# Placing matmul operands on a 256-byte grid, with the block products' stationary weights 64 bytes further

## Chip, core and metric

The kernel runs on one core of a Trainium2 chip. The metric is the device time of one execution in microseconds; the time given for the kernel before is the median of three runs.

## What is computed

One decoder layer in float32 on 512 tokens of width 1024: a half-step SwiGLU FFN (hidden width 2816), a token mixer (sparse attention beside dilated sliding-window attention, gated), and a second half-step FFN, each between RMS norms:

```python
def swiglu(x, w_gate, w_up, w_down):
    return (jax.nn.silu(x @ w_gate) * (x @ w_up)) @ w_down
...
        h = rms_norm(x, ffn1_pre[l])
        x = x + 0.5 * rms_norm(swiglu(h, ffn1_w_gate[l], ffn1_w_up[l], ffn1_w_down[l]), ffn1_post[l])
        h = rms_norm(x, mix_pre[l])
        y = token_mixer(h, w_in[l], nsa_pe_k[l], nsa_w_ck1[l], nsa_w_ck2[l], nsa_pe_v[l],
                        nsa_w_cv1[l], nsa_w_cv2[l], w_nsa_o[l], w_dil_o[l], w_mix_out[l])
        x = x + rms_norm(y, mix_post[l])
        h = rms_norm(x, ffn2_pre[l])
        x = x + 0.5 * rms_norm(swiglu(h, ffn2_w_gate[l], ffn2_w_up[l], ffn2_w_down[l]), ffn2_post[l])
```

## The kernel before

Every float32 product is made of three faster ones. A matrix is split into a rounded part (hi, of type float32r) and a rest (lo); `mm3` then adds hi x hi, hi x lo and lo x hi into one PSUM bank. These are the three lines L409, L410 and L411 of the profile, one matmul each with a weight load (LDWEIGHTS, the row PEld) of its own. The split of weights costs a cast on ScalarE (L380, whi <- raw) and a subtraction on VectorE (L387, wlo <- raw,whi), both 128 x 1024.

`wpair` hands out the split weights' places: three buffers each of tags whi and wlo, used in turn, 4096 bytes a partition. `wsplit` takes a pair and issues the split. Activations and some weights live in slots (x, ring, W, PT, NN, Q, KA and so on) of 2048 or 4096 bytes, and in xh and xl.

The FFN's two first products are computed two blocks of 128 hidden columns at a time (`strassen`, 9 times in the first FFN and 10 times in the second): VectorE forms sums of weight blocks (L645 to L656, into tmp or raw), and seven block products follow, each on weights from `block` and each of 2 x 4 `mm3` with 256 moving columns (`product`), that is 24 matmuls. In them the weights (whi, wlo) are stationary and the tokens (xh, xl, or sums of them in NN, N, PT, CB) move. In the down projections and in the mixer's projection of its output (`ffn_down`, `down`) the activations are stationary and whi and wlo move, 512 columns at a time or, in some products of the mixer, 256. In the remaining projections the weights are stationary and 256 or 512 token columns move.

VectorE also forms sums of the down projection's weights between the block products (L758). The order of all instructions on each engine is written out by hand in a table (`ORDER`), and the tables `HOMES` say which buffer of a tag each use takes. Weights come in by DMAs on SP's queue into three raw buffers.

The pool places each tile at its first use, one after another in steps of 32 bytes in a partition. The small tiles ss, rs and rs2 (4 bytes a partition, for the norms; eight, four and four buffers) were first used between larger ones, and so moved the larger ones off a common place. In the built program the start addresses modulo 256 bytes are:

| tile | before | after |
|---|---|---|
| x, raw, xh, xl, SP, ring, W, NN, N, PT, CB, V, KB, Q, KA, of | 160 | 160 |
| whi, wlo buffer 0 | 96 | 160 |
| whi, wlo buffer 1 | 160 | 160 |
| whi, wlo buffer 2 | 32 | 160 |
| whi, wlo as `block` uses them | 96, 160, 32 | 224 |
| tmp | 96 | 160 |

Column blocks of 128 elements are 512 bytes, so a place modulo 256 holds for all k and j of a tile.

Of the kernel before, what the change touches and what calls it, by code (L numbers as in the profile page):

```python
# [13 lines left out]
F32 = mybir.dt.float32  # L14
F32R = mybir.dt.float32r
# [7 lines left out]
P = 128  # L23
# [164 lines left out]
HOMES = dict(  # L188
    x=(
        "0765432107654321076543120756431207564312075643120756431207563421706534217065342170653421"  # L190
    ),
    raw=(
        "021021021021021021021021021021021021021021021201201210212101201201201202102102102102102102102102"
        "10210210210210210210210210210"
    ),
    SP=(
# [6 lines left out]
    ss=(  # L203
        "076512347056124371023417052643714073150427136540"
    ),
    rs=(
        "031203120312031203120312"
    ),
    rs2=(
        "031203120312031203120312"  # L210
    ),
# [83 lines left out]
            8: ["of"] * 2 + ["V"] * 2, 9: ["KB"] * 4}  # L295
STEPS = (2, 2, 2), (4, 2)
EARLY = 5
HOLD_TAGS = ["W"] * 2 + ["Q"] * 4 + ["KA"] * 2 + ["V"] * 2 + ["CB", "ring"]
PS_BUFS = dict(S=3, T=2, V=1, F=2)
PS_TAGS = [t for t in PS_BUFS for _ in range(PS_BUFS[t])]  # L300
# [7 lines left out]
class Layer:  # L308
    def __init__(self, ctx, tc, a):
        self.tc, self.nc, self.a = tc, tc.nc, a  # L310
        self.pool = ctx.enter_context(tc.tile_pool(name="sb", bufs=1))
        self.psum = ctx.enter_context(tc.tile_pool(name="ps", bufs=1, space=PSUM))
        self.nps = 0
        self.whole = {}
        self.made = {}
        self.consts()

    def behind(self, ins):
        return nullcontext() if ORDER else self.tc.issue_after(ins)
# [43 lines left out]
        self.nc.sync.dma_start(r, src)  # L363
        return r

    def wpair(self, shape):
        n = 1
        for s in shape:
            n *= s
        out = []  # L370
        for tag in ("whi", "wlo"):
            w = self.tile(self.pool, [P, 1024], F32R, tag, tag, 3)[:, :n]
            if len(shape) == 2:
                w = w.rearrange("p (a b) -> p a b", b=shape[1])
            out.append(w)
        return out
# [22 lines left out]
    def ktiles(self, w):  # L399
        return [[v[:, k] for k in range(KT)] for v in w]  # L400

    def wsplit(self, src, shape, behind=None):
        hi, lo = self.wpair(shape)
        self.split(hi, lo, src, behind)
        return hi, lo

# [163 lines left out]
    def ffn(self, n, wg, wu, wd, post, finish, xsrc, tags, nps, aside=None):  # L570
# [10 lines left out]
        def unit(m, f, slots=False):  # L581
            w = {"g": wg, "u": wu}[m]
            if self.pre_split:
                return self.pre_split.pop(0)
            if f % 2 == 0:
                raws[m] = self.raw(w[:, f * P:(f + 2) * P].rearrange("(k p) f -> p k f", p=P), [KT, 2 * P])
            src = raws[m][:, :, (f % 2) * P:(f % 2 + 1) * P]
            if slots:
                return self.wslots(src, "SP", (self.last_cast, self.last_update) if n else None)
            return self.ktiles(self.wsplit(src, [KT, P]))  # L590
# [16 lines left out]

        def block(src):

            return self.wsplit(src, [4, 2 * P])  # L610

        def product(b, w, rhs, start, stop):
            for j in range(2):
# [5 lines left out]
        def strassen(p):  # L619
# [24 lines left out]

            nc.vector.tensor_add(s1, a21, a22)  # L645
            w = block(a11)
            nc.vector.tensor_sub(a21, a11, a21)
            product(r11, w, b11, True, False)
            w = block(a21)
            product(r7, w, t3, True, True)  # L650
            nc.vector.tensor_sub(s2, s1, a11)
            w = block(s2)
            nc.scalar.copy(r12, r11)
            product(r12, w, t2, False, False)
# [27 lines left out]
        for tag, (m, f) in zip(tags, todo):  # L682
            w = unit(m, f, len(first) == 3)
# [32 lines left out]
        for p in range(NF // 2):  # L716
# [26 lines left out]
            hi, lo = [self.slot(tags["E"].pop(0), F32R) for _ in range(2)]  # L743
# [92 lines left out]
    def ffn_down(self, E, X, Y, wd, post, finish, xsrc, defer):  # L836
# [27 lines left out]
        def product(a, wname, banks, start, stop, side=None, tail=0, keep=None, between=None, pre=(), begin=0, end=NP):  # L864


            held = []

            def mm(t, k, w):
                hi, lo = a(k, t)  # L870
                self.mm3(banks[t], hi, lo, w[0], w[1], start and k == 0, stop and k == end - 1, True)

            for k, w in pre:
                for t in range(2):
                    mm(t, k, w)
            for k0 in range(begin, end, 4):
                n = min(4, end - k0)
                r = self.raw(weights[wname](k0, n), [n, S])
                for k1 in range(0, n, 2):
                    m = min(2, n - k1)  # L880
                    if keep and k0 + k1 + m > end - tail:
                        for j in range(m):
                            w = [self.slot(keep.pop(0), F32R) for _ in range(2)]
                            self.split(w[0], w[1], r[:, k1 + j])
                            held.append((k0 + k1 + j, w))
                        continue
                    hi, lo = self.wsplit(r[:, k1:k1 + m], [m, S])
                    for j in range(m):
                        k = k0 + k1 + j
                        if k >= end - tail:  # L890
                            held.append((k, (hi[:, j], lo[:, j])))
                        else:
                            for t in range(2):
                                mm(t, k, (hi[:, j], lo[:, j]))
                        if side:
                            side(k)
            for t in range(2):
                for k, w in held:
                    mm(t, k, w)
                if t == 0 and between:  # L900
                    between()

        def half(lst, off):
            return lambda k, t: [v[:, off + t * P:off + (t + 1) * P] for v in lst[k]]
# [39 lines left out]
        else:  # L944
            nc.sync.dma_start(xl[:, 0:EARLY].bitcast(F32), weights["T4"](0, EARLY))

        def held_sums(k):
            ks = slice(k, min(k + 2, EARLY))
            src = xl[:, ks].bitcast(F32)
            if defer:  # L950
                d4 = self.sbt("tmp", [P, 2, S], bufs=2)[:, 0:ks.stop - k]
                with self.behind(self.last_rest):
                    nc.vector.tensor_sub(d4, xh[:, ks].bitcast(F32), src)
                src = d4
            self.split(xh[:, ks], xl[:, ks], src)

        todo = list(range(0, EARLY, 2))

# [33 lines left out]
        def between():  # L992
            scaled(2, 0, c[0])
            r = self.rstd([ms[2, 0], ms[2, 1]], 2.0)
            while self.pending:
                self.pending.pop(0)()
            update(2, (c[0], c22[0]), r)

        product(half(parts["O"], 256), "T4", c, False, True, None, NP - EARLY, list(HOLD_TAGS), between,
                [(k, (xh[:, i], xl[:, i])) for i, k in enumerate(defer or range(EARLY))],  # L1000
                *((3, NP - 2) if defer else (EARLY, NP)))
        r = self.rstd([self.meansq(c[1], S, 2.0), ms[3, 1]], 2.0)
# [903 lines left out]
```

## Time and profile before

| | |
|---|---|
| median of three runs | 1118.34 us (1118.12 to 1118.46) |
| the profiled execution | 1118.38 us |
| its span, first to last instruction | 1116.3 us |
| TensorE busy | 1107.4 us, 99%, 7070 matmuls |
| VectorE busy | 916.6 us, 82% |
| ScalarE busy | 654.0 us, 59% |
| granted TensorE clock, mean | 0.999 |

Matmuls are pipelined: the duration of one in the profile overlaps the next one's. How fast TensorE gets through a stretch is read from the starts of its matmuls, first to last, divided by their number. A row of the timeline gives start in us, duration in us, engine, line, operation, tiles (out <- operands: the moving one first, the stationary one second), shape and count.

### The profile page before, as it was taken

What the parts mean: (1) busy time and instruction counts of PE and PEld (TensorE: products, weight loads), DVE (VectorE), ACT (ScalarE), POOL (GpSimd) and SP (SyncE); (2) the same over time, 40 slices, a digit from 0 to 9 for tenths busy, and PEclk for the clock granted to TensorE, in tenths of its full rate; (3) what the DMA queues carried; (4) which work ended last, traced back from release to release, by engine and by line L of the source; (5) the groups of instructions that cost most, each with busy time, mean ns of one, the idle gap of its engine ahead of it and who ended that gap; (6) DMA issues with size and microseconds to landing.
All of it is one profiled execution on the core that took longest, in us unless ns stands there. A gap on an engine that the chain in (4) does not pass through costs nothing.

```text
span 1116.3 us, 18832 instructions
## 1 busy us (share of the span) xinstructions
PE 1107.4 (99%) x7070; PEld 1000.2 (90%) x7070; DVE 916.6 (82%) x1569; ACT 654.0 (59%) x1185; POOL 78.8 (7%) x112
## 2 busy tenths in 40 slices
PE   9999999999999999999999999999999999999997
PEld 8899999998889988888888998888999999998886
DVE  7799999988787878987666688976898988879674
ACT  6355555566564777887564725645655555558462
POOL 1000000000002022443000000001000000000001
PEclk9999999999999999999999999999999999999999
DMA  9967676788864562202467768782324334257862
GB/s 294 305 200 243 217 227 191 220 279 284 309 197 119 167 164 85 92 14 71 167 206 263 222 179 289 238 283 95 105 86 130 127 123 133 88 198 239 281 219 81
DMA packets 153952, 207.36 MB, mean 186 GB/s; under 512 B 19939, under 2 KB 98563, under 8 KB 153605
## 3 DMA queue, kind: packets, MB, share of 16 engines
q1 hardware_dynamic: 153856, 206.16, 57.0%
q8 instruction: 55, 0.90, 0.3%
q14 instruction: 37, 0.30, 0.1%
q10 hardware_dynamic: 4, 0.00, 0.0%
HBM read 166.76 MB, written 39.37 MB: 185 GB/s over the span
## 4 chain that ended last, share of the span: by engine, by line
PE 92%; DVE 3%; DMA 2%; ACT 1%; issue 1%; POOL 1%; SPq 0%; DVEq 0%; POOLq 0%; ACTq 0%
PE pb_F L409 12%; PE pb_F L411 12%; PE pb_F L410 11%; PE pb_S L409 8%; PE pb_S L411 8%; PE pb_S L410 8%; PE pb_T L409 6%; PE pb_T L411 6%; PE pb_T L410 6%; PE pb_V L409 3%; PE pb_V L410 3%; PE pb_V L411 3%; PE pb_V L1340 2%; PE pb_T L1325 2%; PE pb_S L1059 1%; DMA raw<-in_w_in_dram 1%
## 5 line engine op out<-in xcount | busy, mean ns | idle before, releaser
L380 ACT CAST whi<-raw 128x1024 fp32r<-128x1024 f32 (+1 forms) x213 | 217.2, 1022 | 246.2 <-issue 75.7
L387 DVE TENSOR_TENSOR wlo<-raw,whi 128x1024 fp32r<-128x1024 f32 (+1 forms) x213 | 252.6, 1188 | 95.0 <-ACT whi L380 86.6
L409 PE MATMUL pb_F<-xh_t,whi 128*128 128x512 f32 (+1 forms) x392 | 142.1, 364 | 0.1
L411 PE MATMUL pb_F<-xh_t,wlo 128*128 128x512 f32 (+1 forms) x392 | 141.2, 362 | 0.2 <-DVE wlo L387 0.2
L410 PE MATMUL pb_F<-xl_t,whi 128*128 128x512 f32 (+1 forms) x392 | 141.1, 362 | 0.0
L380 ACT CAST whi<-tmp_t 128x1024 fp32r<-128x1024 f32 x58 | 60.8, 1049 | 58.2 <-PE pb_S L410 23.0
L387 DVE TENSOR_TENSOR wlo<-tmp_t,whi 128x1024 fp32r<-128x1024 f32 x58 | 70.9, 1222 | 19.5 <-ACT whi L380 18.8
L409 PEld LDWEIGHTS pb_F<-xh_t,whi 128*128 128x128 f32 x392 | 73.9, 189 | 10.0 <-issue 0.3
L411 PEld LDWEIGHTS pb_F<-xh_t,wlo 128*128 128x128 f32 x392 | 73.9, 189 | 9.9 <-DVE wlo L387 0.6
L410 PEld LDWEIGHTS pb_F<-xl_t,whi 128*128 128x128 f32 x392 | 73.9, 189 | 9.0
L409 PE MATMUL pb_S<-xh_t,whi 128*128 128x256 f32 (+1 forms) x232 | 67.3, 290 | 0.0
L411 PE MATMUL pb_S<-xh_t,wlo 128*128 128x256 f32 (+1 forms) x232 | 67.0, 289 | 0.0
L410 PE MATMUL pb_S<-xl_t,whi 128*128 128x256 f32 (+1 forms) x232 | 66.8, 288 | 0.0
L1316 POOL TENSOR_SCALAR SP_s<-SP_s,st_t 128x384 f32<-128x384 f32 (+2 forms) x48 | 49.4, 1043 | 100.6 <-DVE wlo L387 50.8
L431 POOL TENSOR_TENSOR rs_t<-rs_t,mhalf_t 128x1 f32<-128x1 f32 x24 | 15.5, 647 | 536.5 <-DVE rs_t L427 536.0
L411 PE MATMUL pb_T<-xh_t,wlo 128*128 128x256 f32 x184 | 51.7, 283 | 0.0
L410 PE MATMUL pb_T<-xl_t,whi 128*128 128x256 f32 x184 | 51.1, 281 | 0.0
L409 PE MATMUL pb_T<-xh_t,whi 128*128 128x256 f32 x184 | 51.1, 283 | 0.0
L387 DVE TENSOR_TENSOR PT_s<-pb_T,PT_s 128x512 fp32r<-128x512 f32 (+1 forms) x72 | 39.7, 560 | 6.1 <-ACT PT_s L380 5.4
L1065 DVE CUSTOM_DVE_ANT_0 SP_s<-pb_S,W_s 128x128 f32<-128x128 f32 (+2 forms) x92 | 38.7, 444 | 7.3 <-PE pb_S L1060 5.0
L411 PEld LDWEIGHTS pb_S<-xh_t,wlo 128*128 128x128 f32 x232 | 43.8, 189 | 0.7
L409 PEld LDWEIGHTS pb_S<-xh_t,whi 128*128 128x128 f32 x232 | 43.8, 189 | 0.7
(858 smaller groups left out, 3472.0 us busy)
## 6 DMA issues: line engine op xcount, KB each, us to landing
raw<-in_ffn_w_up_dram SPq DMA_DIRECT2D x40, 512.0 KB, 4.4
raw<-in_ffn_w_gate_dram SPq DMA_DIRECT2D x39, 512.0 KB, 4.9
raw<-in_w_in_dram SPq DMA_DIRECT2D x18, 1024.0 KB, 5.5
raw<-in_ffn_w_down_dram SPq DMA_DIRECT2D x14, 1024.0 KB, 5.8
raw<-tdram SPq DMA_DIRECT2D x14, 1024.0 KB, 5.1
NN_s<-in_ffn_w_down_dram SPq DMA_DIRECT2D x22, 512.0 KB, 4.4
tdram<-NN_s SPq DMA_DIRECT2D x22, 512.0 KB, 4.1
odram<-ring_s SPq DMA_DIRECT2D x38, 128.0 KB, 3.3
```

Of the source, the lines that this page charges most:

```text
L380: self.last_cast = self.nc.scalar.copy(dsthi, src).ins
L387: self.last_rest = self.nc.vector.tensor_sub(dstlo, src, dsthi.bitcast(F32)).ins
L409: mm(out, lhi, rhi, start=start, stop=False, skip_group_check=skip)
L410: mm(out, lhi, rlo, start=False, stop=False, skip_group_check=skip)
L411: mm(out, llo, rhi, start=False, stop=stop, skip_group_check=skip)
L431: nc.gpsimd.tensor_tensor(out=r, in0=v, in1=self.mhalf, op=OP.pow)
L1059: mm(out, q[:, qc], ka[:, kc], start=True, stop=False)
L1065: nc.vector.tensor_tensor_reduce(p, s, w, -1.0, FLOOR, OP.add, OP.min, st_m)
L1316: nc.gpsimd.tensor_scalar(pp, pp, st[:, 1, t:t + 1], None, op0=OP.mult)
L1325: nc.tensor.transpose(b[:, o + (t - kk) * P:o + (t - kk + 1) * P], pt[pn][:, po + kk * P:po + (kk + 1) * P], self.ident)
L1340: self.nc.tensor.matmul(out[:, kk * P:S], v, pp, start=first and kk == 0 and pi == 0, stop=False, skip_group_check=True)
```

## The change

The tiles of ss, rs and rs2 are placed first of all. The buffers of whi and wlo are 1088 elements wide in place of 1024 (4352 bytes, 17 times 256), and `block` takes its pair 16 elements (64 bytes) into the buffer. The order of instructions on each engine, their operations and shapes, and their waits are the same as before.

```diff
+SHIFT = 16
...
         self.consts()
+        for tag in ("ss", "rs", "rs2"):
+            for place in sorted(set(HOMES.get(tag, ""))):
+                self.pool.tile([P, 1], F32, name=tag + "_t", tag=tag + place, bufs=1)
...
-    def wpair(self, shape):
+    def wpair(self, shape, shift=0):
...
-            w = self.tile(self.pool, [P, 1024], F32R, tag, tag, 3)[:, :n]
+            w = self.tile(self.pool, [P, 1088], F32R, tag, tag, 3)[:, shift:shift + n]
...
-    def wsplit(self, src, shape, behind=None):
-        hi, lo = self.wpair(shape)
+    def wsplit(self, src, shape, behind=None, shift=0):
+        hi, lo = self.wpair(shape, shift)
...
         def block(src):
-            return self.wsplit(src, [4, 2 * P])
+            return self.wsplit(src, [4, 2 * P], None, SHIFT)
```

## The prediction

> **What bounds the kernel now.** I read the page first (busy shares, granted clock, the chain that ended last), then the table by stretches of 50 us, then the order in time of TensorE alone, to see how far apart its matmuls start.
>
> ```profile
> span 1116.3 us, 18832 instructions
> PE 1107.4 (99%) x7070; PEld 1000.2 (90%) x7070; DVE 916.6 (82%) x1569; ACT 654.0 (59%) x1185; POOL 78.8 (7%) x112
> PEclk9999999999999999999999999999999999999999
> PE 92%; DVE 3%; DMA 2%; ACT 1%; issue 1%; POOL 1%; SPq 0%; DVEq 0%; POOLq 0%; ACTq 0%
> ```
>
> TensorE is 99% busy, its clock is granted in full, and 92% of the chain that ended last is TensorE. So the time is a sum of matmul pitches (start of one to start of the next); the durations in the groups overlap and are of no use for that sum. The sum below is made against the profiled execution's own 1118.38 us (span 1116.3 and 2.1 around it), which stands 0.04 above the median of the three runs, 1118.34.
>
> ```profile
> core 0: us, PE busy (x) PEld busy (x) DVE busy (x) ACT busy (x) POOL busy (x), PEclk, DMA share, GB/s
> 100.00:150.00 50.00, 50.00 (x424) 50.00 (x423) 48.72 (x64) 27.39 (x39) 0.00 (x0) 1.00 0.70 229
> 250.00:300.00 50.00, 50.00 (x217) 40.50 (x217) 37.15 (x45) 30.65 (x42) 0.00 (x0) 1.00 0.85 297
> 450.00:500.00 50.00, 49.92 (x292) 41.98 (x291) 44.38 (x129) 40.79 (x100) 23.50 (x23) 1.00 0.17 54
> 900.00:950.00 50.00, 50.00 (x424) 50.00 (x423) 44.48 (x56) 27.17 (x37) 0.00 (x0) 1.00 0.40 124
> ```
>
> In the block products of the first FFN (row 100:150) TensorE never stops, and VectorE is 48.72 of 50 us busy as well. In those of the second FFN (row 900:950) VectorE has 5.5 us to spare. The first FFN's down projection (250:300) has matmuls of 512 columns and a full TensorE. In the token mixer (450:500) four engines alternate, so a faster matmul is not sure to end the stretch earlier there.
>
> **The change part by part.** No instruction and no wait is added, removed or moved; only addresses differ. What can change is the pitch of a matmul by where its two operands lie to each other. I call *offset* the stationary operand's address less the moving operand's, modulo 256 bytes. Before, the operands in x, ring and the other slots lie at 160, and the three whi/wlo buffers at 96, 160 and 32, so the kernel goes through offsets 192, 0 and 128 where weights are stationary, and 64, 0 and 128 where they move. The trace of before is thus an experiment on the change.
>
> Block products (19 calls of strassen, 7 products each, 24 matmuls of 256 columns in a product, 3192 in all). Three products that follow each other, each row the first matmul of one, with the weights at 96, 160 and 32:
>
> ```profile
> 184.44 0.28 PE L409 MATMUL pb_S<-NN_s,whi 128*128 128x256 f32 x1
> ...
> 187.27 0.28 PE L409 MATMUL pb_T<-xh_t,whi 128*128 128x256 f32 x1
> ...
> 190.14 0.28 PE L409 MATMUL pb_S<-NN_s,whi 128*128 128x256 f32 x1
> ...
> 192.98 0.28 PE L409 MATMUL pb_T<-NN_s,whi 128*128 128x256 f32 x1
> ```
>
> They take 2.83, 2.87 and 2.84 us, so 117.9, 119.6 and 118.3 ns a matmul, 118.6 on the mean. After the change the offset is 64 in all 3192. No block product of before has that, but 48 matmuls of the mixer's output projection do: 256 columns, moving whi at 96, stationary xh at 160. The rows, first a stretch of offset 64 from 623.99 to 625.01, then 128 up to 626.44, then 64 again:
>
> ```profile
> 623.99 0.28 PE L409 MATMUL pb_F<-whi,xh_t 128*128 128x256 f32 x1
> ...
> 625.01 0.28 PE L409 MATMUL pb_F<-whi,xh_t 128*128 128x256 f32 x1
> ...
> 626.44 0.28 PE L409 MATMUL pb_F<-whi,xh_t 128*128 128x256 f32 x1
> ...
> 627.14 0.28 PE L409 MATMUL pb_F<-whi,xh_t 128*128 128x256 f32 x1
> ...
> 627.83 0.28 PE L409 MATMUL pb_F<-whi,xh_t 128*128 128x256 f32 x1
> ```
>
> From 623.99 to 625.01 are 9 matmuls: 113.3 ns each. The next 12, at offset 128, take 119.2, near the 118.3 that the block product at 128 takes with the roles turned round, so what counts seems to be the offset and not which operand lies where. Coming from another offset, the pattern needs some matmuls to settle: the 12 from 626.44 take 115.8 on the mean, of which the last six 115. After the change every product has the same offset as the one ahead, so I take the settled 113.3. A product then takes 2.720 us for 2.847, and 133 products save 133 x 0.127 = 16.9 us. The bounds are 115.8 (8.9 us) and, against a gain, the slowest of the rows, 119.6 (3.2 us lost).
>
> Matmuls of 512 columns in the same triples (counted in the built program): 948 at offset 0 or within 12 bytes of it, 324 around 64, 636 around 128, 312 at 192; after the change 2220 at 0 or within 12 bytes. Rows for a stretch of each offset, in the order 192 (9 matmuls), 0 (17), 128 (12), 64 (12):
>
> ```profile
> 550.24 0.39 PE L411 MATMUL pb_F<-xh_t,wlo 128*128 128x512 f32 x1
> ...
> 552.29 0.39 PE L411 MATMUL pb_F<-xh_t,wlo 128*128 128x512 f32 x1
> ...
> 618.00 0.39 PE L410 MATMUL pb_F<-xl_t,whi 128*128 128x512 f32 x1
> ...
> 621.85 0.22 PE L1059 MATMUL pb_S<-KA_s,Q_s 128*128 128x128 f32 x1
> ...
> 1009.09 0.40 PE L409 MATMUL pb_F<-whi,KB_s 128*128 128x512 f32 x1
> ...
> 1011.88 0.39 PE L409 MATMUL pb_F<-whi,x_s 128*128 128x512 f32 x1
> ...
> 1014.68 0.40 PE L409 MATMUL pb_F<-whi,x_s 128*128 128x512 f32 x1
> ```
>
> That is 2.05/9 = 228, 3.85/17 = 226.5, 2.79/12 = 232.5 and 2.80/12 = 233.3 ns. For this width offset 0 is the fastest. The saving is 324 x 6.8 + 636 x 6.0 + 312 x 1.5 = 2.2 + 3.8 + 0.5 = 6.5 us. Two things are left out because they are near each other: the matmuls at 0 that now follow another offset and lose a few ns in settling (a gain, at most 2 us by the same few matmuls as above), and the part that lies in the mixer, where other engines may hold the end (a loss of about the same). Bounds: 4.5 and 8.5.
>
> The other products of 256 columns (432 with weights stationary outside the block products, 96 in the output projection) go to offset 0, the slowest of the three: 432 x (119.6 - 118.6) and 48 x 6.3 and 48 x 0.4 is 0.4 + 0.3 + 0.0 = 0.7 us lost.  Scores, transposes and the P V products keep offsets or change in a few dozen matmuls: nothing, from -0.5 to 0.5.
>
> The cover that shrinks is VectorE's in the first FFN. One call of strassen, from its wlo to the same wlo of the next, with the rows that hold a wait, and one product's wlo with its first use:
>
> ```profile
> 156.08 1.22 DVE L387 TENSOR_TENSOR wlo<-raw,whi 128x1024 fp32r<-128x1024 f32 x1
> ...
> 159.06 0.28 PE L411 MATMUL pb_S<-xh_t,wlo 128*128 128x256 f32 x1
> ...
> 160.03 1.23 DVE L387 TENSOR_TENSOR wlo<-tmp_t,whi 128x1024 fp32r<-128x1024 f32 x1 [0.40 <-ACT whi L380]
> 161.17 0.69 DVE L678 TENSOR_TENSOR ring_s<-ring_s,W_s 128x512 f32<-128x512 f32 x1
> 161.77 0.42 DVE L387 TENSOR_TENSOR x_s<-ring_s,x_s 128x256 fp32r<-128x256 f32 x1
> ...
> 173.01 1.22 DVE L387 TENSOR_TENSOR wlo<-tmp_t,whi 128x1024 fp32r<-128x1024 f32 x1
> 174.26 1.23 DVE L651 TENSOR_TENSOR tmp_t<-tmp_t,raw 128x1024 f32<-128x1024 f32 x1
> ...
> 178.87 0.69 DVE L676 TENSOR_TENSOR ring_s<-ring_s,W_s 128x512 f32<-128x512 f32 x1
> 179.94 1.23 DVE L387 TENSOR_TENSOR wlo<-tmp_t,whi 128x1024 fp32r<-128x1024 f32 x1 [0.39 <-ACT whi L380]
> ```
>
> A call's period is 19.91 us. Back to back, a 1024-wide subtraction takes VectorE 1.14 (160.03 to 161.17) and a 512-wide one 0.60 (161.17 to 161.77). So 0.47 are lost ahead of 179.94 and 0.11 ahead of 174.26, both on ScalarE, which in turn waits for TensorE to free a weight buffer: VectorE needs 19.33. TensorE will need 168 x 0.1133 = 19.03. VectorE falls behind by 0.30 in each of the 9 calls of the first FFN, 2.7 us in all. Its lead for the tightest product is 159.06 - 157.30 = 1.76 us. So TensorE should begin to wait for wlo in the sixth or seventh call, 0.9 us in all; the bounds are 0 (the last call has fewer sums) and 2.7 (no lead is left). In the second FFN 44.48/50 x 19.91 = 17.7 us is under 19.03: nothing there. The wlo rows, of different buffers, all have 1.22 or 1.23 us, so I cost VectorE's and ScalarE's own operations at nothing; DMA at 0.70 and 0.40 of its time takes 4 to 5% more rate.
>
> Sum: 16.9 + 6.5 - 0.7 - 0.9 = 21.8 us, 1118.38 - 21.8 = 1096.6.
>
> **The rivals.** First, VectorE takes over the whole stage in the first FFN: if the lead of 1.76 us is not usable, each of 9 calls takes 19.33, and the stage gives up 2.7 for 0.9: 1098.4; with 19.4 (48.72/50 of 19.91) it is 1099. For it speaks the 48.72 of 50; against it that its waits were for ScalarE.
>
> Second, the 512-wide part is lost behind other waits: 16.9 - 0.7 - 0.9 = 15.3, 1103.1. Against it: of the stretches that carry it, a large part is FFN down projection, where TensorE is full (250:300).
>
> Third, the block products don't settle (waits shift the pattern at each product): 115.8 ns, 8 us less, 1104.6. Against it: at one offset, nothing changes from product to product.
>
> Fourth, places don't matter and the three pitches belong to something else that goes round with the buffers, such as which product it is: 0 us, 1118.4. Against it: in one stretch of like matmuls, from 623.99 to 627.83, the pitch goes from 113.3 to 119.2 and back as the buffer changes. The Trainium skill's page "SBUF — State Buffer", section "Who interferes with whom", would have it so: it gives TensorE one read port for the moving operand and an independent one for weight loads, and says that PE and ACT never wait on anyone; by it the sum is 0. The trace does not agree, with 113.3 against 119.2 ns in one product.
>
> Fifth, the other side: the stationary operand now lies at 224, where none of before's weights lie, and the pattern depends on that place as well as on the offset. From 118.6 + (6.5 - 0.7)/3192 = 120.4 ns on, the kernel is slower. At 123 ns, about 3.4 above the slowest product seen, it is 3192 x 4.4 = 14.0 lost, 5.8 won: 1126.6. Against it: 128 gives 118.3 and 119.2 with the operands at 160/32 and 32/160.
>
> **How the numbers follow.** Forecast 0.72, VectorE 0.09, 512-wide part lost 0.06, not settled 0.05, no effect 0.03, slower 0.05. Predicted is the forecast, 1096.6. Its own range is 1093.5 (8.5 for the 512-wide matmuls, no wait for VectorE: 24.7 us) to 1099.5; the range given goes from 1093 to 1103.2, which takes in the first two rivals (0.87). About 0.2%, 2.2 us, is what a measurement of this kernel can tell from no change: faster 0.92, same 0.03, slower 0.05.
>
> **What would show it.** In the profile after: products of 24 matmuls 2.72 us apart in both FFNs, 512-wide triples 226 to 227 ns apart throughout, the clock still full; in the first FFN's block products a VectorE over 99% busy, and TensorE waits on wlo only in the last third. Wrong it would be if products stayed at 2.83 to 2.87 (no effect of place), if they went over 2.89 (the place itself counts), or if those of the first FFN took 2.76 from the first call on (VectorE).

## The result and the profile after

The changed kernel takes 1111.27 us (median of 4 runs, 1110.08 to 1111.73), the kernel before on the same chip 1118.32 (1118.12 to 1118.46): a ratio of 0.9935, with a 95% interval of 0.9918 to 0.9953. It is faster, but by 7 us and not by 22. The profiled execution took 1111.73 us. The lines of its page that answer to those of before:

```profile
span 1109.6 us, 18832 instructions
PE 1100.2 (99%) x7070; PEld 998.0 (90%) x7070; DVE 915.6 (83%) x1569; ACT 654.0 (59%) x1185; POOL 79.0 (7%) x112
PEclk9999999999999999999999999999999999999999
PE 91%; DVE 3%; DMA 2%; ACT 1%; issue 1%; POOL 1%; SPq 0%; DVEq 0%; POOLq 0%; ACTq 0%
```

The same bound, the same clock, 7.2 us less of a busy TensorE. The table by stretches tells where (columns as before):

```profile
100.00:150.00 50.00, 50.00 (x427) 50.00 (x426) 49.26 (x65) 28.30 (x40) 0.00 (x0) 1.00 0.72 231
250.00:300.00 50.00, 50.00 (x221) 41.24 (x221) 38.08 (x46) 31.07 (x42) 0.00 (x0) 1.00 0.87 300
900.00:950.00 50.00, 50.00 (x426) 50.00 (x426) 45.04 (x55) 28.06 (x39) 0.00 (x0) 1.00 0.39 119
```

In 50 us of block products TensorE does 427 and 426 matmuls for 424 before, where 113.3 ns would give some 443 (50/0.1133, and about two that reach over the ends of the window). In the down projection it does 221 for 217. VectorE is busy 49.26 of 50 in the first FFN, where over 49.5 was to show that it had become the bound. In the order in time of TensorE, the first matmuls of three products (line numbers are 4 higher than before):

```profile
184.76 0.28 PE L413 MATMUL pb_S<-NN_s,whi 128*128 128x256 f32 x1
...
187.59 0.28 PE L413 MATMUL pb_T<-xh_t,whi 128*128 128x256 f32 x1
...
190.42 0.28 PE L413 MATMUL pb_S<-NN_s,whi 128*128 128x256 f32 x1
...
193.24 0.28 PE L413 MATMUL pb_T<-NN_s,whi 128*128 128x256 f32 x1
```

2.83, 2.83 and 2.82 us: 117.8 ns a matmul, in these and in every other settled product of both FFNs. The differences from buffer to buffer are gone, as the change would have it, but the common value is 117.8, not 113.3. The other two kinds of matmul, 51 of 256 columns in the mixer and 33 of 512 columns in the second FFN's down projection, both now at offset 0 (first row and the row after the last of each). The 256-wide ones are what the prediction calls the output projection; in the kernel they are the mixer's projection to values (`C_VD`), with xh stationary and whi moving.

```profile
621.22 0.28 PE L413 MATMUL pb_F<-whi,xh_t 128*128 128x256 f32 x1
...
627.34 0.28 PE L413 MATMUL pb_F<-whi,xh_t 128*128 128x256 f32 x1
...
1004.80 0.39 PE L413 MATMUL pb_F<-whi,KB_s 128*128 128x512 f32 x1
...
1012.28 0.39 PE L413 MATMUL pb_F<-whi,of_s 128*128 128x512 f32 x1
```

6.12/51 = 120.0 ns and 7.48/33 = 226.7 ns, near the prediction's 119.6 and 226.5.

Since both kernels have the same matmuls in the same order, the start of each in one trace can be taken from its start in the other. How that difference grows, by stretch of the trace of before (us, negative is gained):

| stretch | what | after | best_mix | once_light |
|---|---|---|---|---|
| 0 to 59.2 | start, input | +1.21 | +0.37 | +0.20 |
| 59.2 to 238.5 | block products, first FFN | -1.24 | -5.35 | -7.86 |
| 238.5 to 329.2 | down projection, first FFN | -1.68 | -1.70 | -1.70 |
| 329.2 to 804.1 | token mixer, second FFN's entry | -1.83 | -2.46 | -3.03 |
| 804.1 to 1003.4 | block products, second FFN | -1.39 | -8.71 | -8.71 |
| 1003.4 to the last matmul | down projection, second FFN | -1.73 | -1.70 | -1.70 |

The last two columns are experiments below. The 1.2 us lost at the start of this execution is a DMA of the input that landed later (ScalarE begins the norm of its fourth block at 7.49 us, before at 6.25); at that place the experiments' executions, with the same instructions at the start, lie between 0.1 and 1.8 behind before, so it belongs to the execution and not to the change. So the 512-wide matmuls brought nearly what was forecast, and the block products brought 2.6 us instead of 16.9. The experiments ask why matmuls of before settled at 113.3 ns at offset 64 and 3192 at the same offset do not.

### The profile page after: what moved, and what is told of

It reads as the page before. It is cut to its first block, busy times and chain, and to the rows that moved or that the text cites. A ratio compares the mean times of both kernels' runs of the same rounds, so it can differ in the third digit from the quotient of the medians.

```text
span 1109.6 us, 18832 instructions
## 1 busy us (share of the span) xinstructions
PE 1100.2 (99%) x7070; PEld 998.0 (90%) x7070; DVE 915.6 (83%) x1569; ACT 654.0 (59%) x1185; POOL 79.0 (7%) x112
## 4 chain that ended last, share of the span: by engine, by line
PE 91%; DVE 3%; DMA 2%; ACT 1%; issue 1%; POOL 1%; SPq 0%; DVEq 0%; POOLq 0%; ACTq 0%
PE pb_F L413 12%; PE pb_F L415 12%; PE pb_F L414 11%; PE pb_S L415 8%; PE pb_S L414 8%; PE pb_S L413 8%; PE pb_T L413 6%; PE pb_T L415 6%; PE pb_T L414 6%; PE pb_V L414 3%; PE pb_V L413 3%; PE pb_V L415 3%; PE pb_V L1344 2%; PE pb_T L1329 2%; PE pb_S L1063 1%; DMA raw<-in_w_in_dram 1%
## 5 line engine op out<-in xcount | busy, mean ns | idle before, releaser
L391 DVE TENSOR_TENSOR wlo<-tmp_t,whi 128x1024 fp32r<-128x1024 f32 x58 | 70.9, 1222 | 17.3 <-ACT whi L384 16.9
L414 PEld LDWEIGHTS pb_S<-xl_t,whi 128*128 128x128 f32 x232 | 44.1, 190 | 0.6
```

The source lines that it names most:

```text
L391: self.last_rest = self.nc.vector.tensor_sub(dstlo, src, dsthi.bitcast(F32)).ins
L414: mm(out, lhi, rlo, start=False, stop=False, skip_group_check=skip)
```

## Experiments

Experiments of one group below ran on one chip, beside the kernel before on that chip.

**Offset by offset, at three places, and the grid alone.** Three sweeps give each call of strassen (and each product of a down projection) an offset of its own, in the same order; they differ only in where the moving operands lie, at 160, 96 or 0, moved by a pad tile. A fourth kernel keeps the grid and drops the shift.

```diff
-SHIFT = 16
+BLOCK_SHIFTS = [0, 8, 16, 24, 32, 40, 48, 56, 16, 4, 12, 20, 28, 36, 44, 52, 60, 16, 48]
+DOWN_SHIFTS = [16, 32, 48, 8, 24, 40, 0, 56, 4, 12, 20, 28, 36, 0]
...
+        self.pool.tile([P, 48], F32, name="pad", tag="pad", bufs=1)   # sweep_at96; 24 wide in sweep_at0; none in sweep_at160
...
-            return self.wsplit(src, [4, 2 * P], None, SHIFT)
+            return self.wsplit(src, [4, 2 * P], None, self.block_shift)
...
+            self.block_shift = self.block_shifts.pop(0)
```

grid_only is `SHIFT = 0` in the changed kernel.

> The changed kernel, but each of the 19 calls of strassen places its weights at a step of its own (0, 32, 64, 96, 128, 160, 192, 224 and 64 bytes in the first FFN; 16, 48, 80, 112, 144, 176, 208, 240, 64 and 192 in the second), and each product of the FFN down projections has a shift of its own for the moving weights. Moving operands of the block products at 160. Read are the pitches per call, not the time. Theory 'place' (the pitch depends on where both operands start, so 113.3 ns needs the moving one at 96 and the stationary one at 160): 117.7 ns at offset 64 again in both FFNs, 120.0 at 0, about 118.5 at 128, 117.7 at 192. Theory 'role' (113.3 belongs to products with activations stationary): the same four numbers, so it is told apart by the next run. Theory 'finer offset' (only the distance counts, and 64 is not its best value for this width): some offset that is no multiple of 64 falls under 116 ns.

> The same sweep with 192 bytes put ahead of all larger tiles, so that the moving operands lie at 96 and weights with offset 64 at 160, as in the mixer's 113.3 ns stretch. Theory 'place': 113.3 ns a matmul at offset 64 in the calls of both FFNs. Theory 'role': 117.7 ns there, and the whole curve over the offset as with the moving operands at 160, within 0.3 ns. Theory 'finer offset': the curve as at 160, too.

> The same sweep with 96 bytes put ahead, moving operands at 0. Theory 'place' with a line of 64 bytes (160 and 96 both start in the middle of a line of 64): another curve, lower by 2 to 6 ns at some offsets. If only the distance counts: the curve of the two other sweeps within 0.3 ns.

> The changed kernel with SHIFT = 0: one place for all operands, the block products at offset 0. By the pitches read in the two traces (120.0 ns at 0, 117.7 at 64, 118.6 the mean of before): 3192 x 2.3 ns = 7.3 us slower than the changed kernel, about 1118.6 us, equal to before within 1.5 us (512-wide matmuls gain some 6, block products lose 4.5). If the shift of 64 bytes does nothing: 1111 us.

Measured: 1116.35, 1115.24 and 1116.33 us (one run each); the grid alone 1117.84 (1117.46 to 1118.44), a ratio of 0.9997 (0.9987 to 1.0006). The settled pitch of a 256-wide matmul with stationary weights, the mean over the last third of a call's 168, was the same within 0.1 ns in the three sweeps:

| offset, bytes | 0 | 16 | 32 | 48 | 64 | 80 | 96 | 112 | 128 |
|---|---|---|---|---|---|---|---|---|---|
| ns | 120.0 | 118.3 | 118.3 | 123.4 | 117.8 or 113.3 | 118.8 | 117.3 | 120.0 | 118.6 |

| offset, bytes | 144 | 160 | 176 | 192 | 208 | 224 | 240 |
|---|---|---|---|---|---|---|---|
| ns | 120.0 | 120.0 | 118.1 | 117.75 or 113.3 | 116.7 | 117.8 | 120.0 |

So the place itself does not count, only the distance: the prediction's fifth rival is out for these three places. Nor is it that weights that stand still cannot reach 113.3. At offset 64 (and 192) there are two settled values, and both occur in one execution. The order in time of TensorE in the first sweep, two calls at 64: the one that follows a call at 32, and the one that follows a call at 224:

```profile
100.96 0.28 PE L415 MATMUL pb_T<-xh_t,whi 128*128 128x256 f32 x1
...
103.79 0.28 PE L415 MATMUL pb_V<-NN_s,whi 128*128 128x256 f32 x1
...
117.92 0.28 PE L415 MATMUL pb_S<-xh_t,whi 128*128 128x256 f32 x1
...
220.12 0.28 PE L415 MATMUL pb_T<-xh_t,whi 128*128 128x256 f32 x1
...
222.85 0.28 PE L415 MATMUL pb_V<-NN_s,whi 128*128 128x256 f32 x1
...
236.45 0.28 PE L415 MATMUL pb_S<-xh_t,whi 128*128 128x256 f32 x1
```

The six products from 100.96 to 117.92 take 16.96/144 = 117.8 ns a matmul, the five from 222.85 to 236.45 take 13.60/120 = 113.3. The same tiles at the same offset. The starts repeat every three matmuls: 118, 118, 117 ns in the one, 113, 114, 113 in the other. In all three sweeps 64 came out slow after 32, fast after 224 and after 240; 192 slow after 160 and fast behind a fast 64. In the changed kernel both stretches follow matmuls at offset 0, and both come out slow. The other offsets were entered in one way only in these sweeps, so more than one value there is not ruled out.

The grid alone is worth nothing, since the block products then all lie at offset 0, and the 512-wide gain is spent on them; the first matmuls of two of its products:

```profile
183.16 0.28 PE L413 MATMUL pb_V<-NN_s,whi 128*128 128x256 f32 x1
...
186.04 0.28 PE L413 MATMUL pb_S<-NN_s,whi 128*128 128x256 f32 x1
```

2.88/24 = 120.0 ns. What the 64 bytes add to the grid is 6.6 us, as 3192 x (120.0 - 117.8) = 7.0 would have it.

**Entering the stretch in another way.** If the pattern depends on how a stretch at 64 begins, a few products at another offset ahead of it choose the pattern for all that follow. These kernels give each of the 133 block products its own shift (60 is offset 240, 8 is 32, 16 is 64; the first 63 products are the first FFN's):

```diff
-SHIFT = 16
+SHIFTS = [60] * 7 + [16] * 56 + [60] * 7 + [16] * 63       # enter_call: the first call of each FFN at 240
+SHIFTS = [60] * 1 + [16] * 62 + [60] * 1 + [16] * 69       # enter_once: the first product of each FFN
+SHIFTS = [8] * 7 + [16] * 56 + [8] * 7 + [16] * 63         # enter_slow: the first call of each FFN at 32
+SHIFTS = ([60] + [16] * 6) * 19                            # enter_each: the first product of each call
...
-            return self.wsplit(src, [4, 2 * P], None, SHIFT)
+            return self.wsplit(src, [4, 2 * P], None, self.shifts.pop(0))
```

> The changed kernel, but the first call of strassen in each FFN has its weights at offset 240, all others at 64 as there. In the sweeps a call at 64 that followed one at 240 ran at 113.3 ns, one that followed a call at 32 at 117.8. Theory 'two patterns' (at offset 64 the pitch has two settled patterns, 113.3 and 117.7 ns, and the one in which a run of products starts is kept): 120 ns in 2 calls, 113.3 in 17, so 17 x 168 x 4.4 ns = 12.6 us won and 2 x 168 x 2.3 = 0.8 lost against the changed kernel's 1111.3: 1099.5 us, up to 1100.5 if TensorE waits for VectorE in the first FFN. Rival 'waits reset it' (any wait of TensorE for weights throws it back): 117.7 ns again after a few products, about 1110 us. Rival 'chance': the two patterns come and go, 1105 us with a wide spread.

> As enter_call, with only the first product (24 matmuls) of each FFN's first call at offset 240. Theory 'two patterns': the fast one is kept from the second product on if 24 matmuls at 240 set the same start as 168 do: 131 x 24 x 4.4 ns = 13.8 us, 1097.5 to 1098.5 us. If the start depends on where in its own cycle the stretch at 240 ends, one or both FFNs stay slow: about 1104 or 1111 us.

> As enter_call, with offset 32 in the first calls in place of 240. Theory 'two patterns': 118.3 ns in 2 calls and 117.7 in the other 17, 1111.5 us, the changed kernel's time. If any other offset ahead of 64 gives the fast pattern: 1099 us.

> The first product of each of the 19 calls at offset 240, the six others at 64. Theory 'two patterns': each call starts anew, 114 products x 24 x 4.4 ns = 12.0 won, 19 x 24 x 2.3 = 1.0 lost: 1100.3 us if all go fast, and calls in which the start falls otherwise stay at 117.7, which the trace shows call by call.

| kernel | us | ratio (95%) | first FFN, ns a matmul | second FFN |
|---|---|---|---|---|
| enter_call | 1100.37 (1099.59 to 1103.49) | 0.9845 (0.983 to 0.986) | 113.3 from 81 to 138 us, then 117.8 | 113.3 |
| enter_once | 1101.04 (1100.45 to 1101.76) | 0.9846 (0.9832 to 0.9861) | 113.3 from 63 to 117 us, then 117.8 | 113.3 |
| enter_slow | 1107.90 (1105.89 to 1108.34) | 0.9904 (0.9887 to 0.992) | 113.3 from 80 to 175 us but for one product, then 117.8 | 117.8 |
| enter_each | 1100.06 (one run) | | 113.3 in each call, with waits | 113.3 |

Each row of pitches is from one execution; enter_call's is the slowest of its four, 1103.49 us, so the others need not have left the fast pattern at the same place. enter_once came out 2.5 us over what was expected: both FFNs went into the fast pattern, but the first did not stay in it.

One product of 24 matmuls at another offset, 2.8 us long, sets the pace of the 69 products behind it. Three product starts in enter_once's second FFN, the third one three products after the second:

```profile
920.17 0.28 PE L414 MATMUL pb_V<-xh_t,whi 128*128 128x256 f32 x1
...
922.89 0.28 PE L414 MATMUL pb_T<-NN_s,whi 128*128 128x256 f32 x1
...
931.05 0.28 PE L414 MATMUL pb_S<-xh_t,whi 128*128 128x256 f32 x1
```

2.72 us for the first, 8.16 for the next three: 113.3 ns, some 130 us after the only entry there. enter_slow is half a miss: after the call at 32 the second FFN is slow, as in the sweeps, but the first FFN came out fast. So the offset ahead does not decide alone. That it is where in its cycle the pattern ahead stands as the new offset begins would fit, but no run here shows it.

Offset 240 has more than one value, too. The first call of enter_call, seven products at 240, takes 117.3 ns in the first FFN and 120.0 in the second; the entry products take 117.2 to 117.5 without a wait, but 119.5 as the first of a second FFN. Both kinds led into the fast pattern.

In the first FFN the fast pattern was always lost for good on the way where no new entry came. In enter_once it goes at 117.6 us. TensorE's rows there, with the first and the later products:

```profile
111.61 0.28 PE L414 MATMUL pb_T<-NN_s,whi 128*128 128x256 f32 x1
...
114.33 0.28 PE L414 MATMUL pb_S<-xh_t,whi 128*128 128x256 f32 x1
114.44 0.28 PE L415 MATMUL pb_S<-xl_t,whi 128*128 128x256 f32 x1
114.66 0.39 PE L416 MATMUL pb_S<-xh_t,wlo 128*128 128x256 f32 x1
...
117.27 0.28 PE L414 MATMUL pb_S<-xh_t,whi 128*128 128x256 f32 x1
117.38 0.28 PE L415 MATMUL pb_S<-xl_t,whi 128*128 128x256 f32 x1
117.65 0.38 PE L416 MATMUL pb_S<-xh_t,wlo 128*128 128x256 f32 x1
...
120.34 0.28 PE L414 MATMUL pb_S<-NN_s,whi 128*128 128x256 f32 x1
...
185.36 0.28 PE L414 MATMUL pb_T<-xh_t,whi 128*128 128x256 f32 x1
...
188.18 0.28 PE L414 MATMUL pb_S<-NN_s,whi 128*128 128x256 f32 x1
```

Twice the third matmul of a product, the first that uses wlo, starts 0.22 and 0.27 us behind the second, where 0.11 is the pace. After the first of these gaps the fast pattern goes on (from 114.88 to 117.27, 21 matmuls at 113.8); after the second the product ends at 117.8, and so does every one behind it (185.36 to 188.18: 2.82 us). The weight load of that matmul, and VectorE's wlo for both, in the same execution:

```profile
117.65 0.19 PEld L416 LDWEIGHTS pb_S<-xh_t,wlo 128*128 128x128 f32 x1 [0.19 <-DVE wlo L392]
```

```profile
113.39 1.22 DVE L392 TENSOR_TENSOR wlo<-tmp_t,whi 128x1024 fp32r<-128x1024 f32 x1
114.64 1.22 DVE L656 TENSOR_TENSOR tmp_t<-tmp_t,raw 128x1024 f32<-128x1024 f32 x1
...
116.38 1.22 DVE L392 TENSOR_TENSOR wlo<-raw,whi 128x1024 fp32r<-128x1024 f32 x1
117.51 0.68 DVE L680 TENSOR_TENSOR W_s<-W_s,pb_T 128x512 f32<-128x512 f32 x1
```

VectorE ends wlo at 114.61 and 117.60, and the matmuls follow 50 ns later; VectorE itself has no wait in these rows. It has run out of lead, because at 113.3 ns TensorE is the faster of the two.

The length of the gap alone does not decide. In enter_slow's first FFN a gap of much the same size, 0.21 us from the third matmul at 153.37 to the fourth, puts the next 21 matmuls into the slow pattern, and the gaps of 0.18 and 0.22 in the product behind bring the fast one back:

```profile
153.37 0.38 PE L416 MATMUL pb_S<-xh_t,wlo 128*128 128x256 f32 x1
153.58 0.28 PE L414 MATMUL pb_S<-xh_t,whi 128*128 128x256 f32 x1
...
156.06 0.28 PE L414 MATMUL pb_S<-xh_t,whi 128*128 128x256 f32 x1
...
157.28 0.28 PE L414 MATMUL pb_S<-xh_t,whi 128*128 128x256 f32 x1
...
158.98 0.28 PE L414 MATMUL pb_S<-NN_s,whi 128*128 128x256 f32 x1
```

From 153.58 to 156.06 are 21 matmuls, 118.1 ns each, from 157.28 to 158.98 15 of 113.3. At 172.81 the same execution has a gap of 0.21 at the same place of a product once more, and the fast pattern goes on behind it.

**The two causes apart.** once_light is enter_once with VectorE's sums of down weights cut to 64 of their 512 columns, so that VectorE keeps up at the fast pace; after_light is the same cut in the changed kernel.

```diff
-            self.nc.vector.tensor_sub(out, x, y)
+            self.nc.vector.tensor_sub(out[:, :64], x[:, :64], y[:, :64])
```

best_mix has an entry in every call of the first FFN and one in the second, all_208 takes the fastest offset of the sweep that had only one value:

```diff
-SHIFT = 16
+SHIFTS = ([60] + [16] * 6) * 9 + [60] + [16] * 69          # best_mix
+SHIFT = 52                                                 # all_208
```

> One product per FFN at offset 240, then 64 (1101.0 us), and VectorE's sums of down weights take 64 columns in place of 512 (the rest of these sums is left out), which frees about 4 x 0.45 = 1.8 us of VectorE in each call of the first FFN: its need falls from 19.33 to 17.5 us, below TensorE's 19.03. Theory (a wait of TensorE for wlo, as VectorE runs out of lead, throws it out of the fast pattern): 113.3 ns in all 63 products of the first FFN, no product with a gap over 200 ns; 6.5 calls x 168 x 4.4 ns = 4.8 us less, 1096.2 us. Rival (the fast pattern ends there for another reason, such as a DMA or the length of the run): 117.7 ns again from about 115 us on, 1100 to 1101 us.

> The changed kernel with the same shortened sums (64 of 512 columns, the rest left out), no entry product. Theory (the pattern depends on how the stretch is entered; VectorE alone does not choose it): products stay at 117.7 ns in both FFNs, 1110 to 1111.3 us. Rival (VectorE is what holds the block products of the first FFN at 117.7): 113.3 ns in the first FFN, about 1104.8 us.

> First FFN: each call of strassen begins with one product at offset 240 (as in the run with such a product in all 19 calls, 1100.1 us); second FFN: one such product at its start only (as in the run with one product per FFN). Theory (two settled patterns at offset 64, the fast one kept until TensorE waits): the second FFN needs no new entry, since nothing waits there, and saves 9 products x 24 x 4 to 6.7 ns = 0.9 to 1.4 us of the 1100.1: 1098.7 to 1099.2 us. Rival (the pattern is also lost now and then without a wait, so a new entry in each call is needed in both FFNs): some calls of the second FFN at 117.7 ns, 1100 to 1104 us.

> The block products' weights at offset 208 in place of 64. In the three sweeps a call at 208 took 116.67 ns a matmul each time. Theory (208 has one settled pattern): 3192 x (117.75 - 116.67) = 3.4 us less than the changed kernel's 1111.3, so 1107.8 us, with every product at 116.7. Rival (208 too has several patterns, by how it is entered): another pitch, such as 113.3 (1097) or 118 to 120 ns (1112 to 1118 us).

| kernel | us | ratio (95%) | first FFN, ns a matmul | second FFN |
|---|---|---|---|---|
| once_light | 1096.22 (1095.65 to 1097.4) | 0.9804 (0.9788 to 0.982) | 113.3 throughout | 113.3 |
| after_light | 1111.24 (1111.1 to 1111.37) | 0.9935 (0.9915 to 0.9955) | 117.8 throughout | 117.8 |
| best_mix | 1099.38 (1098.81 to 1100.51) | 0.983 (0.9815 to 0.9845) | 113.3, with a wait in most calls | 113.3 |
| all_208 | 1106.77 (1106.02 to 1107.88) | 0.9896 (0.9881 to 0.991) | 116.7 | 116.7 |

With a lighter VectorE, no product of the first FFN waits or leaves the fast pattern. The stretch 100:150, and the first matmuls of three products 120 us after the entry:

```profile
100.00:150.00 50.00, 50.00 (x443) 50.00 (x443) 47.07 (x69) 28.89 (x40) 0.00 (x0) 1.00 0.72 240
```

```profile
184.60 0.28 PE L414 MATMUL pb_S<-NN_s,whi 128*128 128x256 f32 x1
...
187.32 0.28 PE L414 MATMUL pb_T<-NN_s,whi 128*128 128x256 f32 x1
...
190.04 0.28 PE L414 MATMUL pb_S<-xh_t,whi 128*128 128x256 f32 x1
```

443 matmuls in 50 us, 2.72 us a product. VectorE does more instructions (69 for 65 in the changed kernel) in less time. And a lighter VectorE alone does nothing: after_light is the changed kernel's time, 117.8 ns in each of its products. So for the forecast's pace throughout the first FFN both are needed, an entry into the fast pattern and a VectorE that does not fall behind.

best_mix is the fastest version that computes the whole layer: 11.9 us under the changed kernel's 1111.27, 19.2 under the 1118.6 of the kernel before on its chip. It is just above what was expected (1098.7 to 1099.2). Its second FFN gains the full 8.71 us of the table above; its first FFN 5.35 of the 7.86 that once_light shows to be there. The rest is VectorE's: in it a call takes 19.1 us (entry product at 78.69 to the next at 97.83) as long as there is lead, and after that 19.46 (four calls from 116.97 to 194.80), which is VectorE's pace and no longer TensorE's: VectorE is busy 77.69 of those 77.83 us. The entry products of the first FFN that do not wait take 117.5 ns, 24 x 4.2 = 0.1 us each.

all_208 took 116.7 ns in every product of both FFNs, as the sweeps' calls at 208 did, so 208 has shown one pattern only, entered in these few ways; its time is 1.0 below the expected 1107.8, which lies within its own runs. The first matmuls of two products:

```profile
183.13 0.28 PE L413 MATMUL pb_S<-NN_s,whi 128*128 128x256 f32 x1
...
185.93 0.28 PE L413 MATMUL pb_T<-xh_t,whi 128*128 128x256 f32 x1
```

2.80/24 = 116.7.

## Why the prediction was wrong

The forecast was 1096.6 us, in a range of 1093 to 1103.2; the time was 1111.27. The sign was right, the size was a third.

**The step that failed** is "After the change every product has the same offset as the one ahead, so I take the settled 113.3." The premise held: all products have one pitch. But an offset of 64 has two settled pitches, and the nine matmuls from 623.99 showed one of them. Sized with the other, the term is 3192 x (118.6 - 117.75) = 2.7 us in place of 16.9, and the table by stretches has 1.24 + 1.39 = 2.6. The 14.2 us between the two make up nearly all of the 14.7 by which the forecast missed. The trace of before has no 256-wide matmul settled at 117.8 at offset 64: all four of its stretches of twelve there end at 113.3, the six matmuls from 627.14 too (their starts in full are 627.145 and 627.825; the prediction's 115 for them comes of the rounding of the rows). So the reading was right, and what failed was to carry it. A pitch seen in stretches of 12 matmuls, entered from offset 128 or from the scores, was carried to runs of 1512 and 1680 that begin behind offset 0. The third rival, 115.8, allowed for a pattern that does not settle, not for one that settles elsewhere. The term's own outer bound, 119.6, takes in 117.8, but the range of the whole, up to 1103.2, did not go so far. What makes a stretch that follows offset 0 take the slow pattern stays open.

**What counts is the offset:** right, and more exactly than the trace of before could show (three places, the same curve within 0.1 ns). The Trainium skill's page "SBUF — State Buffer", section "Who interferes with whom", has weight loads and moving operands on independent read ports. Taken to mean that neither waits for the other, that rule would make the sweep flat. It goes from 113.3 to 123.4 ns, and the measurement decides.

**512-wide matmuls,** 6.5 us: 226.7 ns in the settled stretches of the down projections, and the two give 1.68 + 1.73 = 3.4. The mixer gives 1.8 net; with the two stretches there in which 256-wide matmuls lose (345 to 375 us: 0.22, the projection to values: 0.27, together the 0.5 of a predicted 0.7) that is 2.3. So about 5.7, within the bounds of 4.5 and 8.5. Not all 2220 came to 226.5: the 96 of the projection to values with 512 columns (637.85 to 660.41 us; stationary xh read at every fourth element, offsets 0, 4, 8 and 12) take 235.0 ns, where the same ones took 237.7 before. The prediction had counted them with the rest.

**VectorE in the first FFN,** 0.9: it did not show, since TensorE never became fast enough. Where the experiments made it fast, it came earlier than worked out: enter_once waits for wlo at 114.6 us, at the end of the third call, not in the sixth or seventh. VectorE's need is not 19.33 us a call but about 19.5 (19.46 in best_mix); the second value in the first rival, 19.4 from the busy share, was nearer. And the one call read, from 160 us, does not stand for the first ones. The first two calls and the third in the trace of before:

```profile
59.18:79.12 19.94, 19.94 (x169) 19.93 (x168) 19.83 (x26) 11.47 (x15) 0.00 (x0) 1.00 0.62 197
79.12:99.05 19.93, 19.93 (x171) 19.93 (x170) 19.86 (x26) 11.39 (x16) 0.00 (x0) 1.00 0.74 240
99.05:118.96 19.91, 19.91 (x171) 19.91 (x170) 19.34 (x25) 10.58 (x14) 0.00 (x0) 1.00 0.70 225
```

In the first two VectorE has 0.1 us to spare and not 0.6. In enter_once the wlo of a call's seventh product is ready 1.45, 0.64 and 0.05 us ahead of its use in the first three calls, 0.8 lost in the second of them and 0.6, up to the wait, in the third, where the prediction had 0.30 a call. And the price of the wait was not the wait, 0.2 to 0.3 us, but the pattern: each of the 41 products behind the second gap costs 24 x 4.45 ns more, 4.4 us in all. With the two products that wait (0.6 us) that is the 5.0 us by which the first FFN of once_light is shorter in the traces (7.86 gained for 2.91), and near the difference of the times (1101.04 and 1096.22).

**Operations on VectorE and ScalarE, DMA, clock:** no change, as costed. A slip that decides nothing: with 24.7 us won, the fast end is 1093.7, not 1093.5.

With both conditions met, once_light, which leaves out most of a sum, comes to 1096.2. So the forecast was of a kernel that the change alone does not give.

## What to carry to other kernels

A pitch that depends on addresses may have more than one settled value: before a short stretch is carried to a long one, look for the same addresses elsewhere in the trace at another pace, and time a long run. Where matmuls with a weight load each run back to back, sweep the distance of their two operands modulo 256 bytes in one kernel, a value per stage, and try a short entry at another distance. And a wait of 0.3 us can cost far more than itself where it ends a pattern that does not come back.

## What the runs showed of the hardware

- The pitch of a weight load and matmul pair (float32r, 128 rows) goes by the distance of the two operands modulo 256 bytes: 113.3 to 123.4 ns at 256 columns. At 512 columns in the sweeps, with the weights moving, 0 was the best with 226.7, 192 gave 228.9, the other offsets 231 to 234.
- At 64 and 192 two cycles of three matmuls are both stable, 113, 114, 113 and 118, 118, 117 ns, the slow one over all 133 products of the changed kernel. Which one is taken depends on how the stretch begins; a single product at offset 240 ahead led into the fast one each time (33 entries in four kernels). Offset 240 settled at 117.3 and at 120.0.
- A wait may end the fast cycle, leave it, or bring it back. With no new entry behind it, gaps of 0.26 to 0.27 us ended it for good (one each in enter_call, enter_once and enter_slow). A gap of 0.21 to 0.22 left it in enter_once at 114.44 and in enter_slow at 136.92 and 172.81, and ended it for one product in enter_slow at 153.37; gaps of 0.18 and 0.22 in the next product brought it back. So the length alone does not decide; what does is open.
